# A hybrid attention and retention block on one core: another order of the modulation weights and of the first two token blocks, and later requests for rows and the context copy

## The chip, the cores and the metric

The kernel runs on one core of a Trainium2 chip. The metric is the device time of one execution in microseconds (us). A core has TensorE (PE in the rows, PEld its weight loads), VectorE (DVE), ScalarE (ACT), GpSimd (POOL) and SyncE (SP, which here only issues transfers). Each engine runs its own list of instructions in order; they wait for one another through semaphores.

## The reference

One layer of a diffusion backbone, for 2048 latent tokens and 256 context tokens of width 1024. The part that the change touches is the start: modulation, normalisation and the first columns of the input projection.

```python
mod = jax.nn.silu(c) @ w_ada[i] + b_ada[i]
mod_c = jax.nn.silu(c_ctx) @ w_ada[i] + b_ada[i]
shift, scale, gate = ...
h_lat = _rmsnorm(x, norm_g[i]) * (1.0 + scale) + shift
h_ctx = _rmsnorm(ctx, norm_g[i]) * (1.0 + scale_c) + shift_c
# projections of h_lat and h_ctx by w_in: queries, keys, values, gates
# neighbourhood attention (latent queries also read the context keys), retention,
# one output projection, gated residual, final RMSNorm
```

## The kernel before, in words

All is float32 at the interface. A matrix product runs as three products of rounded halves: an operand is split into a high part (`hhi`, `whi`) and a low part (`hlo`, `wlo`), made by a copy with rounding on ACT and a subtraction on DVE or POOL.

**The front.** The modulation weights come in 16 chunks (u, j) of 0.5 MB; u names a quarter of the channels. `ada_split` splits a chunk, `ada_mm` multiplies it with the silu of c and c_ctx (two rows); a chunk that is not split is multiplied in plain float32 (`silc`, two rows). `ada_row` and `ada_fin` copy the sum of a quarter out, transpose it (`mm<-ident,o`) and write its `mods`. The tokens come in eight blocks of 256 latent tokens (0 to 7) and block 8, the context. For each block `squares` (`sq`) sums squares (ACT, then POOL and DVE into `st`), `colsum` (`cs`) sums over channels on PE (`mm<-one,st`), `rstd` (`rs`) takes the inverse root, `spread` (`sp`) spreads it over partitions on PE (`mm<-ident,t`), `spread_mul` (`mu`) multiplies x by it, `prep_ab` (`ab`) applies scale and shift, `prep_hl` (`hl`) splits into high and low. Blocks 0 and 1 take `prep_first` (`p`, 128 channels k at a time) in place of the last two.

**The windows.** The attention keys (weight columns 512 to 1023, `w01`) are computed in five windows: windows 0 to 3 have two token blocks each, window 4 the context. A window has four units of eight steps, a step being three matmuls (line 363). The results are stored to DRAM as `kS`. The list `PLAN` holds entries (n, action): action is issued once step n has been issued, counted over all windows (32 each); all entries with n = -1 come before the first step. `STEPS` gives the order of units over the steps of window 0 and `LOADS` the order of the first loads. A queue of an engine is thus written out by hand: what stands in `PLAN` between two steps stands between their matmuls on PE.

**The context stage.** After window 4 come four units over context tokens (`CTXU`: weight columns 2560, 2816, 3328, 3072; line 374, 48 matmuls each), whose weights are loaded into `st` and split in turn, and then the latent values. Here stand also: reads of the rows of the first tokens back from DRAM (`raw_piece`, `hhi<-hS` and `hlo<-hS`), and a copy of the context rows to DRAM (`cS`). In window 4 the `kS` stores are issued by ACT, not by SP.

Of the kernel before, what the change touches and what calls it, by code (L numbers as in the profile page):

```python
# [9 lines left out]
F32 = mybir.dt.float32  # L10
# [8 lines left out]
P = 128  # L19
# [39 lines left out]
]  # L59
SPL = [9, 0, 1, 0]  # L60
ALO = [0, 5, 9, 4]
PFL = [3, 0, 0, 1, 0, 3, 1, 3]
STEPS = [0, 1, 2, 0, 1, 3, 2, 3, 2, 0, 3, 1, 1, 3, 0, 3, 2, 3, 0, 0, 2, 1, 1, 1, 1, 2, 3, 2, 2, 0, 3, 0]
WSL = [3, 2]
LEAD = 32
LOADS = [
# [16 lines left out]
def hybrid_kernel(ctx: ExitStack, tc: tile.TileContext, a: dict, out: bass.AP):  # L83
# [24 lines left out]
    sil4 = cst.tile([P, KC, 4], F32R, name="sil4")  # L108
    mods = cst.tile([P, 4, 3, 2, 2], F32, name="mods")
# [145 lines left out]
    def prep_first(k):  # L255
        if k == KC - 1:
            spill.extend((i, u, now[0] + 8) for i in range(2) for u in range(2))
        for i in range(2):
            hi, lo = sub_dst(i)
            A, B = ab(i, k)  # L260
            x = raw[i][k // KH][:, k % KH, :]
            nc.scalar.activation(hi[:, k, :], x, AF.Identity, bias=B, scale=A)
            nc.vector.tensor_scalar(x, x, A, B, ALU.mult, ALU.add)
            eng = nc.gpsimd if PFL[k] >> i & 1 else nc.vector
            eng.tensor_tensor(lo[:, k, :], x, f(hi[:, k, :]), ALU.subtract)
# [27 lines left out]
    def ada_split(u, j):  # L293
        whl[u, j] = []
        for k in range(2):
# [3 lines left out]
            eng = nc.gpsimd if ALO[u] >> j & 1 else nc.vector  # L299
            eng.tensor_tensor(t[:, 1, :], w, f(t)[:, 0, :], ALU.subtract)  # L300
            whl[u, j].append(t)

    def ada_mm(u, j):
        if u not in aps:
            aps[u] = ptile(psm)
        for k in range(2):
            ops = [(silc, wad[4 * u + j][:, k, :])]
# [8 lines left out]
    def ada_row(u):  # L316
        rows[u] = op.tile([P, 2, 512], F32, name="o")[:, 0, :]
        n = 4 if SPL[u] else 2
        (nc.scalar.copy, nc.vector.tensor_copy)[u % 2](rows[u][0:n, :], aps[u][0:n, :])
# [132 lines left out]
    nc.sync.dma_start(silc, a["c2"])  # L452
    nc.scalar.activation(silc, silc, AF.Silu)
    nc.scalar.copy(sil4[:, :, 0:2], silc)
# [10 lines left out]
    for name, *args in LOADS:  # L465
# [4 lines left out]
                ws=lambda g: w01.append(w_split(wr[g], lo=WSL[g])))  # L470
    w01 = []
# [19 lines left out]
    def window(b):  # L491
        units = [u_k(w01, 512 + 256 * g, ct, b) for g in range(2) for ct in range(2)]
        left = [KC] * 4
        for n, u in enumerate(STEPS if b == 0 else [u for u in range(4) for _ in range(KC)]):
            if b == 4 and n == 0:
                env["queue"] = nc.scalar
            if b == 4 and n % 4 == 0:
                raw_piece(n // 4)
            if b == 4 and n == 16:
                wr.append(w_split(wr[2]))  # L500
# [11 lines left out]
    def raw_piece(n):  # L512
        u, k = n // 4, (0, 4, 2, 6)[n % 4]
# [288 lines left out]
    for hl in range(2):  # L802
        nc.sync.dma_start(cS[hl], f(blk[4][hl]))
    for n, (c0, u) in enumerate(CTXU):
# [3 lines left out]
        load_w()  # L808
        unit(u(w0, c0, 8))
# [3 lines left out]
    wo_open()  # L813
# [802 lines left out]
```

## Time and profile before

| what | value |
|---|---|
| three runs | 1373.41, 1373.45, 1375.43 us; median 1373.45 |
| profiled execution | 1372.08 us, span 1370.3 us, so 1.8 us lie around the span |
| window 0, first to last step | 28.1 to 72.7 us |
| window 4 | 150.9 to 162.3 us |
| context units | 162.3 to 196.9 us |

The span runs from the first to the last instruction, and times in rows count from its start. PE is busy in 96% of it, so it is the engine to look at: time in which PE waits, or runs at a lower clock, is time of the kernel, as long as nothing later waits anyway.

### The profile page before, as it was taken

How to read it: one execution, taken by the hardware profiler on the slowest of the kernel's cores; microseconds unless marked ns; L12 is line 12 of the kernel's file. 1: busy time of each engine (PE TensorE's matmuls, PEld its weight loads, DVE VectorE, ACT ScalarE, POOL GpSimd, SP SyncE). 2: the span in 40 equal slices, each digit the busy share in tenths (PEclk: the TensorE clock that was granted, in tenths of full speed). 3: DMA queues.
4: the chain of work that ended last, by engine and by line, in shares of the span. 5: the costliest groups of instructions: out<-in, count | busy, mean ns of one | idle time of the engine just before them, and what ended most of it. 6: DMA issues, size and time to landing. Idle time of an engine off the chain costs nothing.

```text
span 1370.3 us, 23083 instructions
## 1 busy us (share of the span) xinstructions
PE 1313.3 (96%) x8236; PEld 1150.2 (84%) x8236; DVE 826.8 (60%) x1440; ACT 606.5 (44%) x1259; POOL 587.7 (43%) x573
## 2 busy tenths in 40 slices
PE   6989989999999999999999999999999899999997
PEld 2477889887898688998899889889998789888886
DVE  5786246577575665377767777776654633345345
ACT  4454333333532444455556465556642234333332
POOL 4452201445124664445535474655423154444432
PEclk9999999999999999999999999999999999999999
DMA  9386877554868566967687787676538998555533
GB/s 364 129 276 234 292 270 182 176 200 153 312 184 233 216 207 200 277 195 202 166 217 203 208 228 225 173 198 200 156 98 267 273 275 277 169 169 169 161 119 128
DMA packets 197397, 287.25 MB, mean 210 GB/s; under 512 B 17313, under 2 KB 125985, under 8 KB 195746
## 3 DMA queue, kind: packets, MB, share of 16 engines
q1 hardware_dynamic: 164866, 228.35, 55.9%
q10 hardware_dynamic: 32416, 57.42, 11.7%
q8 instruction: 66, 1.08, 0.3%
q14 instruction: 49, 0.40, 0.1%
HBM read 194.48 MB, written 91.23 MB: 208 GB/s over the span
## 4 chain that ended last, share of the span: by engine, by line
PE 51%; DMA 7%; DVE 5%; POOL 3%; ACT 3%; issue 2%; SPq 1%; ACTq 0%; DVEq 0%; POOLq 0%
PE mm L374 12%; PE mm L1457 11%; PE mm L671 5%; PE sS L1017 4%; PE tr L1044 3%; PE mm L363 3%; PE po L1065 3%; PE mm L1180 2%; PE tr L1046 2%; PE po L1067 2%; DMA v<-rvS 1%; PE mm L1369 1%; PE mm L1368 1%; PE mm L1367 1%; DMA woS<-g 1%
## 5 line engine op out<-in xcount | busy, mean ns | idle before, releaser
L374 PE MATMUL mm<-whi,hlo 128*128 128x256 f32 x832 | 228.5, 282 | 0.0
L374 PE MATMUL mm<-whi,hhi 128*128 128x256 f32 x768 | 224.2, 292 | 0.0
L374 PE MATMUL mm<-wlo,hhi 128*128 128x256 f32 x768 | 216.8, 282 | 0.0
L1048 ACT CAST pt<-tr 128x640 fp32r<-128x640 f32 (+1 forms) x128 | 95.7, 747 | 161.7 <-PE tr L1046 159.3
L1054 DVE TENSOR_TENSOR pt<-tr,pt 128x640 fp32r<-128x640 f32 (+1 forms) x128 | 113.9, 890 | 79.1 <-ACT pt L1048 77.9
L374 PEld LDWEIGHTS mm<-whi,hlo 128*128 128x128 f32 x832 | 156.3, 190 | 0.4 <-DMA hlo<-cS 0.3
L1037 POOL TENSOR_SCALAR sp<-sp,stt 128x640 f32<-128x640 f32 (+2 forms) x128 | 103.1, 808 | 106.7 <-DVE stt L1036 80.4
L374 PEld LDWEIGHTS mm<-whi,hhi 128*128 128x128 f32 x768 | 146.2, 190 | 0.0
L374 PEld LDWEIGHTS mm<-wlo,hhi 128*128 128x128 f32 x768 | 146.0, 190 | 0.0
L1026 DVE CUSTOM_DVE_ANT_0 sp<-sS,nb 128x640 f32<-128x640 f32 (+2 forms) x128 | 105.5, 824 | 33.6 <-PE sS L1017 27.2
L1031 ACT ACTIVATE sp<-sp,stt 128x640 f32<-128x640 f32 (+2 forms) x128 | 107.4, 839 | 19.9 <-DVE stt L1026 18.7
L363 PE MATMUL mm<-hlo,whi 128*128 128x512 f32 x256 | 101.2, 395 | 6.6 <-DVE hlo L283 2.3
L625 POOL TENSOR_TENSOR whi<-st,whi 128x512 fp32r<-128x512 f32 x48 | 64.0, 1354 | 101.4 <-ACT whi L624 101.4
L363 PE MATMUL mm<-hhi,whi 128*128 128x512 f32 x256 | 107.0, 418 | 0.0
L1017 PE MATMUL sS<-k,q 128*128 128x256 f32 (+3 forms) x512 | 99.1, 315 | 5.3 <-DVE stt L1026 5.0
L363 PE MATMUL mm<-hhi,wlo 128*128 128x512 f32 x256 | 101.2, 395 | 0.3 <-DVE wlo L347 0.3
L671 PE MATMUL mm<-hhi,whi 128*128 128x512 f32 x336 | 98.2, 395 | 2.6 <-POOL whi L625 2.4
L1457 PE MATMUL mm<-wor,y 128*128 128x512 f32 x384 | 95.7, 398 | 1.9 <-DVE xt L1466 1.1
L1466 DVE TENSOR_TENSOR xt<-mm,xt 128x512 f32<-128x512 f32 x64 | 43.8, 686 | 86.5 <-PE mm L1457 86.4
L1017 PEld LDWEIGHTS sS<-k,q 128*128 128x128 f32 x512 | 82.8, 188 | 12.1 <-DVE stt L1026 8.4
L1457 PE MATMUL mm<-won,y 128*128 128x512 f32 x336 | 89.9, 406 | 0.0
L625 POOL TENSOR_TENSOR wlo<-st,wlo 128x512 fp32r<-128x512 f32 x36 | 53.1, 1474 | 77.7 <-ACT wlo L624 77.7
(258 smaller groups left out, 3065.1 us busy)
## 6 DMA issues: line engine op xcount, KB each, us to landing
st<-in_w_in_dram SPq DMA_DIRECT2D x64, 512.0 KB
q<-qS SPq DMA_DIRECT2D x64, 256.0 KB
hlo<-hS SPq DMA_DIRECT2D x20, 512.0 KB
k<-kS SPq DMA_DIRECT2D x16, 576.0 KB
kS<-o SPq DMA_DIRECT2D x16, 512.0 KB
vB<-o SPq DMA_DIRECT2D x64, 128.0 KB
qS<-o ACTq DMA_DIRECT2D x16, 512.0 KB
woS<-g ACTq DMA_DIRECT2D x32, 256.0 KB
```

The costliest lines, as they stand in the source:

```text
L363: nc.tensor.matmul(pm[:, :n], ww[:, k, cs], h[:, k, :], start=(k == 0 and i == 0), stop=(k == KC - 1 and i == 2))
L374: nc.tensor.matmul(pm[:, t * WG:(t + 1) * WG], h[:, k, o:o + P], ww[:, k, :], start=(k == 0 and i == 0), stop=(k == KC - 1 and i == 2))
L625: nc.gpsimd.tensor_tensor(t[:, 1], r, f(t)[:, 0], ALU.subtract)
L671: nc.tensor.matmul(pm, ww[:, k, :], hh[:, k, :], start=(k == 0 and i == 0), stop=(k == KH - 1 and i == 2))
L1017: nc.tensor.matmul(o, hd["q"][i][:, hl, j * P:(j + 1) * P], k, start=(hl == 0), stop=(hl == 1))
L1026: nc.vector.tensor_tensor_reduce(T["sp"][:, :n], T["s"], nbz[big][:, o:o + n], -1.0, 3e38, ALU.add, ALU.min, T["st"][:, 0:1])
L1031: nc.scalar.activation(sp[:, :n], sp[:, :n], AF.Exp, bias=st[:, 0:1], scale=-1.0, accum_out=st[:, 1:2])
L1037: nc.gpsimd.tensor_scalar(sp[:, :n], sp[:, :n], st[:, 2:3], 0.0, ALU.mult, ALU.add)
L1048: nc.scalar.copy(pt[:, :ng_ + 2, 0, :], tr[:, :ng_ + 2, :])
L1054: nc.vector.tensor_tensor(pt[:, :n, 1, :], tr[:, :n, :], f(pt)[:, :n, 0, :], ALU.subtract)
L1457: nc.tensor.matmul(pm, yy[:, k, :], ww[:, k, sl], start=(k == 0 and i == 0), stop=(k == 3 and i == 2))
L1466: nc.vector.tensor_tensor(xts[t][:, sl], pm, xts[t][:, sl], ALU.add)
```

## The change

1. The start has another order. The modulation weights of quarter 0 are requested ahead of x; other chunks are split ((0,1), (0,3), (3,0) and (3,2) in place of (0,0), (0,3) and (2,0)), and the four of quarter 2 are multiplied unsplit, one after the other. Beside split chunks of its quarter an unsplit one is multiplied with `silz`, silc with two rows of zeros. The tables that gave each split its engine are gone (`ALO`, `PFL`, `WSL`), and the weights `w01` are split half by half.
2. The units of window 0 go round evenly, and `PLAN` has another order up to step 23; from the entry (23, 'cs', 4) on it is the same.
3. In window 4 only the four pieces of `hhi` are read; those of `hlo` follow between the loads of the context units. The context copy is written later, in halves. The split of the 2560 weights takes DVE and not POOL for its low part. `wo_open` (the first gate weights) moves into the values.

```diff
 PLAN = [
...
-    (4, 's', 2, 0), (4, 'x', 4), (4, 'p', 2), (5, 'sq', 2), (7, 'm', 2, 0), (8, 'm', 2, 1), (9, 'p', 3),
...
-    (12, 'p', 5), (12, 'm', 3, 1), (12, 'p', 4), (13, 'sq', 4), (13, 'cs', 2, 3), (13, 'm', 3, 2), (14, 'm', 3, 3),
...
+    (7, 'm', 2, 0), (7, 'm', 2, 1), (7, 'm', 2, 2), (7, 'm', 2, 3), (7, 'sq', 2), (7, 'sq', 3), (7, 'cs', 2, 3),
...
+    (16, 'ab', 2, 0), (17, 'blk', 1), (17, 'ab', 3, 0), (18, 'hl', 2, 0), (19, 'hl', 3, 0), (20, 'sq', 4), (20, 'ab', 2, 1),
+    (21, 'ab', 3, 1), (22, 'hl', 2, 1), (23, 'hl', 3, 1),
...
-SPL = [9, 0, 1, 0]
+SPL = [10, 0, 0, 5]
...
-            if b == 4 and n % 4 == 0:
-                raw_piece(n // 4)
+            if b == 4 and n % 8 == 0:
+                raw_piece(0, n // 8)
             if b == 4 and n == 16:
-                wr.append(w_split(wr[2]))
+                wr.append(w_split(wr[2], lo=0))
...
-    for hl in range(2):
-        nc.sync.dma_start(cS[hl], f(blk[4][hl]))
+
+    def spill_ctx(hl):
+        for u in range(2):
+            ks = slice(u * KH, (u + 1) * KH)
+            nc.sync.dma_start(cS[hl][:, ks, :], f(blk[4][hl])[:, ks, :])
+
     for n, (c0, u) in enumerate(CTXU):
         if n == 3:
             pump.update(y=0, every=4, q=h_sums(T, 0, 1, frows))
         wn = w_split(wcur.pop(0), lo=0)
         load_w()
+        for m in ((0,), (1,), (2, 3), ())[n]:
+            raw_piece(1, m)
+        if n == 3:
+            spill_ctx(0)
         unit(u(w0, c0, 8))
```

How the instructions move, at three places. On DVE, in window 0: before, the sums of squares of block 4 (`st<-st`) stand ahead of the inverse roots of blocks 2 and 3 and of the modulation of quarter 3 (the last `mods` rows).

```order
L200 TENSOR_TENSOR st<-st 128x512
L201 TENSOR_TENSOR st<-st 128x256
L203 TENSOR_TENSOR st<-st 128x256
L214 TENSOR_SCALAR rs<-mm 128x2
L220 COPY t_447<-rs 128x256
L319 COPY o<-mm 2x512
L214 TENSOR_SCALAR rs<-mm 128x2
L220 COPY t_457<-rs 128x256
L329 TENSOR_TENSOR mods<-mm,bada 128x8
L332 SCALAR_TENSOR_TENSOR mods<-mods,ng 128x4
L241 TENSOR_TENSOR hlo<-hlo,mm 128x1024
```

In the changed kernel the same three sums of block 4 stand on DVE behind quarter 3's `mods` and behind the preparation of blocks 0 to 3:

```order
L329 SCALAR_TENSOR_TENSOR mods<-mods,ng 128x4
L261 TENSOR_SCALAR hhi<-hhi,mods 128x256 x2
L263 TENSOR_TENSOR hlo<-hhi 128x256
L261 TENSOR_SCALAR hhi<-hhi,mods 128x256 x2
L263 TENSOR_TENSOR hlo<-hhi 128x256
L239 TENSOR_TENSOR hlo<-hlo,mm 128x1024 x2
L270 TENSOR_SCALAR hlo<-hlo,mods 128x256 x4
L281 TENSOR_TENSOR hlo<-hlo,hhi 128x4x256
L198 TENSOR_TENSOR st<-st 128x512
L199 TENSOR_TENSOR st<-st 128x256
L201 TENSOR_TENSOR st<-st 128x256
```

So they moved from ahead of that work to behind it; on PE the column sum that needs them, `mm<-one,st`, stays behind step 23 in both kernels.

On PE, around the chunks of quarter 2, which in the changed kernel stand in one piece behind step 7, with the column sums of blocks 2 and 3 right behind them:

```order
L360 MATMUL mm<-hhi,wlo 128x512
L308 MATMUL mm<-hlo,silc 2x512 x8
L207 MATMUL mm<-one,st 128x1 x4
L360 MATMUL mm<-hhi,whi 128x512
L360 MATMUL mm<-hlo,whi 128x512
L360 MATMUL mm<-hhi,wlo 128x512
L321 MATMUL mm<-ident,o 128x2 x4
```

Before, the chunks of quarters 2 and 3 stood one or two at a time between steps, and the column sums of blocks 2 and 3 behind step 13.

On SP, from window 4 on: before, the eight row reads, then the loads of the context units' weights (`st<-in_w_in_dram`) with the context copy between them:

```order
L516 DMA hhi<-hS_88 128x1024 x4
L516 DMA hlo<-hS_87 128x1024 x4
L176 DMA st<-in_w_in_dram 128x1024 x2
L803 DMA cS_93<-chi 128x2048
L803 DMA cS_94<-clo 128x2048
L176 DMA st<-in_w_in_dram 128x1024 x10
```

And in the changed kernel:

```order
L521 DMA hhi<-hS_88 128x1024 x4
L174 DMA st<-in_w_in_dram 128x1024 x4
L521 DMA hlo<-hS_87 128x1024
L174 DMA st<-in_w_in_dram 128x1024 x2
L521 DMA hlo<-hS_87 128x1024
L174 DMA st<-in_w_in_dram 128x1024 x2
L521 DMA hlo<-hS_87 128x1024 x2
L174 DMA st<-in_w_in_dram 128x1024 x2
L811 DMA cS_93<-chi 128x1024 x2
```

Of the requests on this queue, those for the weights of two units (3328 and 3072) now follow the `hhi` reads at once; the `hlo` reads and the copy stand behind them.

## Rows read from the trace of the kernel before

**Rows 1.** The page's head.

```profile
span 1370.3 us, 23083 instructions
```

**Rows 2.** By stage: start:end, us, busy time of the engines (instructions), granted clock, DMA share, GB/s.

```profile
60.40:72.70 12.30, 11.93 (x58) 9.77 (x58) 10.92 (x18) 9.09 (x16) 5.50 (x5) 1.00 0.04 13
72.70:97.60 24.90, 22.56 (x102) 18.20 (x101) 21.56 (x31) 13.68 (x19) 11.33 (x8) 1.00 1.03 339
150.90:162.30 11.40, 11.40 (x98) 11.40 (x97) 1.54 (x3) 3.33 (x5) 2.71 (x2) 1.00 0.96 327
162.30:196.90 34.60, 26.49 (x195) 25.39 (x194) 12.74 (x12) 11.76 (x15) 2.04 (x1) 0.90 0.85 304
188.10:193.60 5.50, 5.00 (x21) 4.71 (x22) 4.04 (x4) 3.52 (x4) 0.00 (x0) 0.50 1.03 396
196.90:420.00 223.10, 223.07 (x1378) 199.83 (x1377) 149.73 (x166) 83.41 (x126) 70.79 (x48) 1.00 0.64 202
```

**Rows 3.** Timeline of PE, 70 to 190: start, us, instruction, [idle before, releaser].

```profile
72.72 0.39 PE L363 MATMUL mm<-hhi,whi 128*128 128x512 f32 x1
75.07 0.47 PE L363 MATMUL mm<-hlo,whi 128*128 128x512 f32 x1 [1.96 <-DVE hlo L283]
...
188.13 0.58 PE L374 MATMUL mm<-whi,chi 128*128 128x256 f32 x1 [5.22 <-ACT whi L345]
```

**Rows 4.** Timeline of SP and its DMA issues, 150 to 200.

```profile
155.49 6.60 SPq L516 DMA_DIRECT2D hlo<-hS  x4
...
168.43 0.42 SPq L803 DMA_DIRECT2D cS<-chi  x1
...
182.57 12.16 SPq L176 DMA_DIRECT2D st<-in_w_in_dram  x8
```

**Rows 5.** Waits of SP's queue, 150 to 200: us in total, times, longest.

```profile
SPq L176 <- DMA kS<-o: 17.5, 2, 12.1
```

**Rows 6.** Timeline of ACT and its DMA issues, 150 to 200.

```profile
168.46 0.52 ACTq L151 DMA_DIRECT2D kS<-o  x1
...
182.59 0.60 ACT L443 ACTIVATE o<-mm 128x512 f32<-128x512 f32 x1 [6.04 <-DMA kS<-o]
...
187.03 1.04 ACT L345 CAST whi<-st 128x1024 fp32r<-128x1024 f32 x1 [3.85 <-DMA st<-in_w_in_dram]
```

**Rows 7.** Timeline of PE: one split chunk of modulation, two unsplit ones.

```profile
35.56 1.09 PE L311 MATMUL mm<-o,sil 128*4 128x512 f32 x4
...
48.08 3.60 PE L311 MATMUL mm<-chi,silc 128*2 128x512 f32 x8
```

**Rows 8.** Timeline of DVE, 56 to 78.

```profile
55.69 0.68 DVE L200 TENSOR_TENSOR st<-st 128x512 f32<-128x512 f32 x1
...
60.41 0.16 DVE L332 SCALAR_TENSOR_TENSOR mods<-mods,ng 128x4 f32<-128x4 f32 x1
...
64.02 0.74 DVE L263 TENSOR_SCALAR hhi<-hhi,mods 128x256 f32<-128x256 f32 x2
64.80 0.85 DVE L265 TENSOR_TENSOR hlo<-hhi 128x256 fp32r<-128x256 f32 x1
65.57 2.34 DVE L241 TENSOR_TENSOR hlo<-hlo,mm 128x1024 f32<-128x1024 f32 x2
...
75.45 2.82 DVE L283 TENSOR_TENSOR hlo<-hlo,hhi 128x1024 fp32r<-128x1024 f32 x1
```

**Rows 9.** Timeline of POOL, 53 to 78.

```profile
53.23 1.44 POOL L200 TENSOR_TENSOR st<-st 128x512 f32<-128x512 f32 x1
54.75 0.73 POOL L201 TENSOR_TENSOR st<-st 128x256 f32<-128x256 f32 x1
...
74.35 2.83 POOL L283 TENSOR_TENSOR hlo<-hlo,hhi 128x1024 fp32r<-128x1024 f32 x1 [1.68 <-ACT hhi L279]
```

**Rows 10.** Timeline of ACT, 64 to 76.

```profile
64.14 2.08 ACT L274 ACTIVATE hlo<-hlo,mods 128x256 f32<-128x256 f32 x4 [1.45 <-DVE hlo L241]
...
73.23 1.99 ACT L279 CAST hhi<-hlo 128x1024 fp32r<-128x1024 f32 x2 [0.64 <-DVE hlo L272]
```

More of the change, by code (lines that the diff above doesn't have):

```diff
@@ L39 @@
 PLAN = [
[19 rows of a table removed]
-]
-SPL = [9, 0, 1, 0]
[L61 to L64, printed above, removed]
[20 rows of a table added]
+]
+SPL = [10, 0, 0, 5]
+STEPS = [0, 1, 0, 1, 2, 3, 2, 3, 0, 1, 2, 3, 0, 1, 2, 3, 0, 1, 2, 3, 0, 1, 2, 3, 0, 0, 1, 1, 2, 2, 3, 3]
 LEAD = 32
 LOADS = [
[3 rows of a table removed]
+    ('a', 0, 0), ('a', 0, 1), ('x', 1), ('a', 0, 2), ('a', 0, 3), ('x', 0), ('c',), ('a', 1, 0), ('a', 1, 1), ('w', 0), ('a', 1, 2),
+    ('a', 1, 3), ('w', 1), ('a', 2, 0), ('a', 2, 1), ('x', 2), ('a', 2, 2), ('a', 2, 3), ('x', 3), ('a', 3, 0), ('a', 3, 1), ('a', 3, 2), ('a', 3, 3),
 ]
@@ L108, in hybrid_kernel @@
     sil4 = cst.tile([P, KC, 4], F32R, name="sil4")
+    silz = cst.tile([P, KC, 4], F32, name="silz")
     mods = cst.tile([P, 4, 3, 2, 2], F32, name="mods")
@@ L257, in prep_first @@
             spill.extend((i, u, now[0] + 8) for i in range(2) for u in range(2))
-        for i in range(2):
+        for i in (1, 0):
             hi, lo = sub_dst(i)
@@ L263, in prep_first @@
             nc.vector.tensor_scalar(x, x, A, B, ALU.mult, ALU.add)
-            eng = nc.gpsimd if PFL[k] >> i & 1 else nc.vector
+            eng = nc.gpsimd if i else nc.vector
             eng.tensor_tensor(lo[:, k, :], x, f(hi[:, k, :]), ALU.subtract)
@@ L298, in ada_split @@
             nc.scalar.copy(t[:, 0, :], w)
-            eng = nc.gpsimd if ALO[u] >> j & 1 else nc.vector
-            eng.tensor_tensor(t[:, 1, :], w, f(t)[:, 0, :], ALU.subtract)
+            nc.vector.tensor_tensor(t[:, 1, :], w, f(t)[:, 0, :], ALU.subtract)
             whl[u, j].append(t)
@@ L306, in ada_mm @@
         for k in range(2):
-            ops = [(silc, wad[4 * u + j][:, k, :])]
+            ops = [(silz if SPL[u] else silc, wad[4 * u + j][:, k, :])]
             if SPL[u] >> j & 1:
@@ L318, in ada_row @@
         n = 4 if SPL[u] else 2
-        (nc.scalar.copy, nc.vector.tensor_copy)[u % 2](rows[u][0:n, :], aps[u][0:n, :])
+        nc.scalar.copy(rows[u][0:n, :], aps[u][0:n, :])
     def ada_fin(u):
@@ L452, in hybrid_kernel @@
     nc.sync.dma_start(silc, a["c2"])
+    nc.vector.memset(silz, 0.0)
     nc.scalar.activation(silc, silc, AF.Silu)
+    nc.vector.tensor_copy(silz[:, :, 0:2], silc)
     nc.scalar.copy(sil4[:, :, 0:2], silc)
@@ L469, in hybrid_kernel, with ws_half @@
                 w2=lambda: load_w(), s=ada_split, m=ada_mm, ar=ada_row, af=ada_fin, p=prep_first,
-                ws=lambda g: w01.append(w_split(wr[g], lo=WSL[g])))
-    w01 = []
+                ws=lambda g, u: ws_half(g, u))
+    w01, wps = [], {}
+    def ws_half(g, u):
+        if u == 0:
+            w, wps[g] = w_parts(wr[g])
+            w01.append(w)
+        wps[g][u]()
     def run_acts(n):
@@ L510, in window, with raw_piece @@
                 tick()
-    def raw_piece(n):
-        u, k = n // 4, (0, 4, 2, 6)[n % 4]
+    def raw_piece(u, n):
+        k = (0, 4, 2, 6)[n]
         if k == 0:
@@ L812, in hybrid_kernel @@
     load_w()
-    wo_open()
-    W, mine = values(vunits([([w0], 1024, 0), ([w0], 1024, 1), ([w1], 1280, 0), ([w1], 1280, 1)]), {}, 4)
+    spill_ctx(1)
+    W, mine = values(vunits([([w0], 1024, 0), ([w0], 1024, 1), ([w1], 1280, 0), ([w1], 1280, 1)]), {0: [wo_open]}, 4)
     def take(b):
```

37 rows, old and new, of tables (LOADS, PLAN) are left out of this document.

## The prediction

> **What bounds the kernel now.** I read the windows by stage first. From 196.9 to 420 PE is busy for 223.07 of 223.10 us [rows 2]: nothing there waits for another engine, so whatever time the two stages before it gain or lose is handed on, not swallowed. The change touches only those stages, the front with its windows and the context stage. Two of their rows show lost time. In the context stage PE is busy for 26.49 of 34.60 us at a granted clock of 0.90 [rows 2]. In the front the losses are small: 11.93 busy of 12.30 us at the end of window 0, then 22.56 of 24.90 us in window 1 and a bit beyond [rows 2], with one wait of 1.96 us for the low part that DVE makes at line 283 [rows 3].
>
> Second the timelines of the context stage. Its worst wait is 5.22 us at 188.13, for ACT's split of the 3072 weights [rows 3]. ACT had waited there for the weights (187.03, [rows 6]), which SP had requested only at 182.57 [rows 4]: SP's queue stood for up to 12.1 us waiting for a `kS` store [rows 5]. ACT issued that store at 168.46 and it was done when ACT itself went on at 182.59 after 6.04 us of waiting for it [rows 6], so it took 14 us. In the same stretch the four `hlo` reads had been put on the queue until 162.1 and the context copy from 168.43 on [rows 4]; DMA was busy at 0.96 and 0.85 [rows 2]. After the wait the granted clock is 0.50, the lower level of 1.2 GHz, for the whole row from 188.10 to 193.60 [rows 2].
>
> **The context stage after the change.** Ahead of the requests for the 3328 and 3072 weights SP now has only the four `hhi` reads; the `hlo` reads (2 MB) and the copy (2 MB) come later. The request for 3072 needs the split of 2816, not the last `kS` store. What is to be gained: window 4 takes 11.40 us for 98 matmuls, 0.116 each, where nothing waits [rows 2]; the 195 matmuls of the stage would then take 22.7 us of its 34.60, so 11.9 us at most. The parts of it that hang on the late request are the 5.22 us and the half of 5.5 us at half clock, 2.75, together 8.0. The rest are shorter waits for weights, behind the same stores. I take 11.0, between 8.0 and 11.9, near the upper end because all the traffic that stood ahead of stores and weights moves together. Where does it go? The copy is read back much later, and the `hlo` reads are wanted in the fourth unit, behind DMA at 0.64 share in the long stage that follows [rows 2]; I price their return at nothing, and if that cover were gone, at the 1.2 us that one 0.5 MB piece takes at the 396 GB/s of [rows 2].
>
> **The front after the change.** *Modulation.* One more chunk is split: 1.09 in place of 1.80 (half of 3.60) on PE [rows 7], so 0.7 less. The first chunk waits for no split any more; at most another 1.09, I take 0.5. Quarter 2's four chunks are 7.2 us in one piece, the same work as before. So quarter 3's modulation comes about when it did (60.41, [rows 8]), 1.2 us earlier.
>
> *The new wait.* Counted from quarter 3's `mods`, PE has ten steps up to step 23, and then the column sum of block 4, whose squares now stand behind everything. PE ran 18 steps in the 11.93 us after 60.4 [rows 2], 0.66 each, so it comes there 6.6 us on. The squares come thus, in DVE's order: four scalings and two low parts, 2 x 0.74 + 2 x 0.85 = 3.2; two `mu` 2.34, in all 5.5 [rows 8]. ACT's four scalings of 2.08 [rows 10] end at 6.6, a cast (half of 1.99, [rows 10]) at 7.6. Then POOL and DVE make one low part each. DVE's row of 75.45 is 2.82 long beside POOL's of 74.35, and ends at 78.27 [rows 8, 9]: the pair takes 3.9 us, since the two do not run at once. That is 11.5. The sums of squares are again POOL's 1.44 and 0.73 [rows 9] and DVE's 0.68 and two shorter ones, which I put at 0.43 each by their size against the 0.68 [rows 8]: 3.7 together if they too take turns, 15.2 in all. PE waits 15.2 - 6.6 = 8.6, and with the 0.5 that its transposes stand ahead of the `mods`, 9 us.
>
> *Behind it.* Eight steps remain, 5.3 us. A wait of 5.22 us left 5.5 us of half clock [rows 2, 3], so a wait of 9 does it too: 2.75. The spreading of block 4, whose inverse root stands on DVE behind four more scalings and a low part, I put at 1 us of waiting, between 0 and the 3.9 of that pair. Window 1 would start 15.2 + 5.3 + 2.75 + 1 = 24.2 after 60.41, at 84.7, against 72.72 before [rows 3]: 12.0 later. Against that stand the 1.2 of the modulation and the 1.96 us of [rows 3], since blocks 2 and 3 are long ready by then: 8.9, say **9 us** lost. The bounds: 6.5, if the clock holds and the spreading waits for nothing (-3.75) but modulation gains nothing (+1.2); 11.5, if modulation comes as much later as two new short waits cost (see the third case).
>
> **The sum.** 1372.08 (the profiled execution; 1.8 us of it lie around the span, [rows 1]) + 9 - 11 = 1370.1. The median of the runs is 1.4 above that execution, so 1371.5. A change of 0.2%, 2.7 us, is about what a measurement of this kernel can tell from none.
>
> **Rivals.**
>
> *The front loses less (faster).* The 9 us rest on POOL and DVE taking turns throughout. For it speaks the pair at 74.35 and 75.45; against it, that scalings and `mu` from PSUM may run beside POOL, and that ACT may be further ahead than I let it. If the wait is 5.2 in place of 9 and the clock still falls, the front loses 5: 1373.45 + 5 - 11 = 1367.5 to 1368.
>
> *The store stays late (slower).* Store and reads are on two queues, ACT's and SP's. What I saw is a store that took 14 us while SP's queue was full; that SP's traffic was the cause is my inference. If the store of the last `kS` unit takes 14 us whatever SP does, ACT stands at the result of the 2816 unit as it did at 182.59, the split of 3072 behind it: PE would wait for it some 5 us again and get the low clock for 2.75, so of the 11 only some 4 are regained: 1373.45 + 9 - 4 = 1378.5. It decides once that store takes more than about 11 us. For it speaks that the stores may simply be slow; against it, that most of the traffic beside them goes away. The Trainium skill has a rule for this: on its page "DMA: Bandwidth & Descriptors", section "Queues, rings and completion order", each DMA engine serves the queues that have work in turn, packet by packet. By that a store on ACT's queue would get its share however long SP's queue is, and emptying SP's queue would help it little. The 14 us of [rows 6] for 0.5 MB don't look like half of the bandwidth, so the trace bears this out only in part.
>
> *A second fall of the clock (about no change).* Right behind quarter 2's chunks PE now has the column sums of blocks 2 and 3, whose squares come from ACT, POOL and DVE only then: a pair of sums costs the 3.7 of above, so two waits of 2 to 2.5 us with almost nothing between them. Single waits of 1.96 us left the clock at 1.00 [rows 2, 3], the 5.22 did not; this lies between. A fall there puts some 5.5 us of chunks and steps at half pace, 2.4 to 2.75 later: 1373.45 + 11.5 - 11 = 1374. The Trainium skill, page "TensorE: Matmul & The Clock Gate", section "HAM oscillation — how this bites in real kernels", says that short work between recurring waits starts at the low clock every time; the waits here are of that kind, and no row before has two in a row.
>
> *It doesn't matter.* That both shifts vanish later is excluded by 223.07 of 223.10 [rows 2].
>
> **How the numbers follow.** The forecast has a chance of 0.35, the cheaper front 0.30, the second fall 0.20, the late store 0.15. The range takes the first three and the lower half of the fourth's way: from 1367.5 (context 11, front 5) to 1377 (context 8, front 11.5). Faster by over 0.2% means below 1370.75: a third of the forecast's case and nearly all of the cheaper front, 0.40. Slower, above 1376.2, are the late store and a little of the others, 0.18. The same is the rest, 0.42.
>
> **What would show it.** PE waits some 9 us for `one,st` of block 4 in window 0, at about 67, released by DVE's last sum of squares, and a stretch of granted clock near 0.5 follows; window 1 starts near 84 and has no wait at its first steps. Quarter 3's `mods` are written between 58 and 61. Window 4 starts 9 us later than 150.9. The context units take 23 to 24 us with a granted clock of 1.00 and no wait over 1.5 us; SP requests the 3072 weights before the last `kS` store has landed. Wrong would be the step on the front if window 1 starts before 80, the step on the context if PE waits there for ACT's split by more than 2 us, and the sum if the stages from 197 on wait for `hlo` reads.

## The result, and the profile after

| | median of runs | profiled execution | first step | window 1 | window 4 | values |
|---|---|---|---|---|---|---|
| before | 1371.85 us (11 runs) | 1372.08 | 28.13 | 72.72 | 150.90 | 196.88 |
| after | 1377.52 us (11 runs) | 1378.85 | 29.38 | 87.93 | 166.89 | 202.45 |

The columns on the right are the starts of the first matmul of a stage on PE's timeline. The ratio is 1.0047, interval 1.0029 to 1.0064: the change makes the kernel 4 to 9 us slower. The forecast was 1371.5, its range 1367.5 to 1377. In the two traces window 4 begins 16.0 us later; the context units take 24.26 us in place of 34.59 and give 10.3 back; 5.6 of loss are left where the values begin, and 6.8 at the end.

The windows by stage of the changed kernel (start:end, us, busy time of PE, PEld, DVE, ACT and POOL with instructions, granted clock, DMA share, GB/s):

```profile
44.00:48.00 4.00, 1.47 (x9) 1.39 (x10) 3.03 (x5) 0.23 (x1) 1.48 (x2) 0.93 0.49 182
48.00:52.00 4.00, 4.00 (x14) 2.95 (x14) 1.99 (x7) 1.61 (x3) 1.06 (x2) 0.50 0.00 0
...
78.30:84.00 5.70, 5.65 (x15) 4.66 (x16) 3.92 (x6) 2.58 (x3) 2.60 (x2) 0.50 0.00 0
...
166.90:178.20 11.30, 11.30 (x98) 11.30 (x97) 3.90 (x5) 3.33 (x5) 0.00 (x0) 1.00 0.95 320
178.20:202.50 24.30, 23.29 (x195) 22.88 (x194) 9.00 (x9) 10.32 (x13) 0.00 (x0) 1.00 0.85 306
202.50:420.00 217.50, 216.82 (x1331) 193.70 (x1331) 147.34 (x165) 83.41 (x125) 69.33 (x47) 1.00 0.68 215
```

Against [rows 2]: the context stage (178.2 to 202.5) has 23.29 us of busy PE in 24.30 at a granted clock of 1.00, where it had 26.49 in 34.60 at 0.90. The values still swallow next to nothing (PE busy for 216.82 of 217.50). In the front there are two stretches at 0.50, 48 to 52 and 78.3 to 84; the kernel before has 1.00 at 48 to 52 and in its row of 60.4 to 72.7 [rows 2].

The timeline of PE in the changed kernel (start, us, instruction, [idle before, releaser]):

```profile
45.03 0.61 PE L207 MATMUL mm<-one,st 128*128 128x1 f32 x4 [1.93 <-DVE st L201]
47.14 0.75 PE L207 MATMUL mm<-one,st 128*128 128x1 f32 x4 [1.50 <-DVE st L201]
...
78.35 1.02 PE L207 MATMUL mm<-one,st 128*128 128x1 f32 x4 [8.28 <-DVE st L201]
...
115.59 0.70 PE L360 MATMUL mm<-hlo,whi 128*128 128x512 f32 x1 [2.83 <-POOL hlo L281]
...
185.54 0.38 PE L371 MATMUL mm<-wlo,chi 128*128 128x256 f32 x1 [0.76 <-DVE wlo L344]
```

The first two waits are the column sums of blocks 2 and 3 behind quarter 2's chunks; the clock falls at the second. The third is the new wait for block 4. The last is the longest of the context units, 0.76 us where [rows 3] had 5.22.

The timeline of DVE in the changed kernel, from quarter 3's `mods` to block 4's sums:

```profile
63.49 0.16 DVE L329 SCALAR_TENSOR_TENSOR mods<-mods,ng 128x4 f32<-128x4 f32 x1
...
72.73 2.50 DVE L281 TENSOR_TENSOR hlo<-hlo,hhi 128x1024 fp32r<-128x1024 f32 x1 [1.48 <-ACT hhi L277]
...
77.87 0.43 DVE L201 TENSOR_TENSOR st<-st 128x256 f32<-128x256 f32 x1
...
81.06 2.55 DVE L281 TENSOR_TENSOR hlo<-hlo,hhi 128x1024 fp32r<-128x1024 f32 x1 [1.47 <-ACT hhi L277]
```

From the `mods` to the end of the sums it is 63.49 to 78.30, 14.8 us, where 15.2 was predicted; but the `mods` come 3.1 later than before [rows 8], not 1.2 earlier. The low part of 81.06, still preparation of blocks 2 and 3, will matter below.

The waits of SP's queue in the changed kernel, 165 to 205 (us in total, times, longest):

```profile
SPq L174 <- DVE wlo L344: 23.4, 10, 7.5
```

the timeline of its issues:

```profile
85.42 0.63 SPq L149 DMA_DIRECT2D kS<-o  x1
...
176.51 10.46 SPq L174 DMA_DIRECT2D st<-in_w_in_dram  x4
```

and that of ACT, both of the changed kernel:

```profile
89.51 0.59 ACT L380 CAST o<-mm 128x512 fp32r<-128x512 f32 x1 [4.19 <-DMA kS<-o]
...
180.28 0.37 ACT L380 CAST o<-mm 128x256 fp32r<-128x256 f32 x1 [4.10 <-DMA kS<-o]
...
182.62 0.52 ACTq L149 DMA_DIRECT2D kS<-o  x1
...
191.29 0.60 ACT L440 ACTIVATE o<-mm 128x512 f32<-128x512 f32 x1 [3.73 <-PE mm L371]
...
199.32 0.59 ACT L446 COPY o<-mm 128x512 f32<-128x512 f32 x1 [5.35 <-DMA rkS<-o]
```

The four requests for the 3328 and 3072 weights are issued from 176.51 on, spread over 10.46 us, and what holds them now is the split that frees their buffers (`wlo`), no longer a `kS` store [rows 5]. The last `kS` store of the stage leaves at 182.62, and at the result of the 2816 unit (191.29) ACT waits for PE, where it had waited for that store [rows 6]. ACT does wait for a store one unit later (199.32), but PE waits for nothing there. The issue at 85.42 stores the first result of window 0.

### The profile page after: what moved, and what is told of

Read it like the earlier page. It is cut to its first block, busy times and chain, and to the rows that moved or that the text cites. A ratio compares the mean times of both kernels' runs of the same rounds, so it can differ in the third digit from the quotient of the medians.

```text
span 1377.1 us, 23099 instructions
## 1 busy us (share of the span) xinstructions
PE 1318.7 (96%) x8236; PEld 1153.9 (84%) x8236; DVE 834.6 (61%) x1445; ACT 608.4 (44%) x1263; POOL 582.8 (42%) x570
## 4 chain that ended last, share of the span: by engine, by line
PE 64%; DMA 10%; DVE 8%; ACT 4%; issue 3%; POOL 3%; SPq 2%; ACTq 0%; DVEq 0%; POOLq 0%
PE mm L371 16%; PE mm L676 13%; PE mm L1470 11%; PE mm L360 5%; PE sS L1030 4%; PE tr L1057 3%; PE po L1078 3%; PE mm L1193 2%; PE tr L1059 2%; PE po L1080 2%; DMA kS<-o 1%; DMA v<-rvS 1%; PE mm L1382 1%; PE mm L1381 1%; PE mm L1380 1%
## 5 line engine op out<-in xcount | busy, mean ns | idle before, releaser
L1039 DVE CUSTOM_DVE_ANT_0 sp<-sS,nb 128x640 f32<-128x640 f32 (+2 forms) x128 | 105.5, 825 | 33.1 <-PE sS L1030 27.7
```

The lines of the kernel that those rows point to most:

```text
L1039: nc.vector.tensor_tensor_reduce(T["sp"][:, :n], T["s"], nbz[big][:, o:o + n], -1.0, 3e38, ALU.add, ALU.min, T["st"][:, 0:1])
```

## The experiments

All fifteen by stage. A profile is one execution; the ratio is that of the timed runs against the kernel before, with its interval. e14 is e6 timed again. The fences with edits show the entries and lines that matter, not the whole difference.

| kernel | first step | window 1 | window 4 | values | context units | ratio |
|---|---|---|---|---|---|---|
| e1, part 3 alone | 28.25 | 74.42 | 153.33 | 189.00 | 24.28 | 0.9954 (0.9935 to 0.9972) |
| e2, parts 1 and 2 | 29.47 | 86.06 | 166.75 | 210.96 | 32.89 | 1.0085 (1.0063 to 1.0107) |
| e6, rows later | 27.24 | 73.45 | 151.41 | 186.85 | 24.05 | 0.9940 (0.9922 to 0.9958) |
| e14, the same | 26.98 | 71.66 | 150.58 | 185.83 | 23.86 | 0.9934 (0.9908 to 0.9960) |
| e7, copy later | 28.00 | 74.25 | 153.37 | 191.60 | 26.85 | 0.9959 (0.9942 to 0.9976) |
| e3, squares early | 28.72 | 86.55 | 164.30 | 200.16 | 24.67 | 1.0028 (1.0012 to 1.0044) |
| e5, filling matmuls | 28.89 | 85.63 | 162.94 | 197.19 | 23.06 | 0.9995 (0.9982 to 1.0008) |
| e3b, sums early too | 29.35 | 74.91 | 161.24 | 196.60 | 24.16 | 1.0020 (1.0007 to 1.0034) |
| e4, and 2, 3 later | 32.72 | 74.95 | 162.68 | 198.66 | 24.78 | 1.0013 (1.0001 to 1.0026) |
| e8, old `STEPS` | 29.04 | 85.17 | 163.88 | 201.35 | 26.27 | 1.0075 (1.0049 to 1.0100) |
| e10, e3b, old `STEPS` | 28.98 | 73.98 | 161.18 | 196.92 | 24.44 | 1.0044 (1.0027 to 1.0060) |
| e9, new start alone | 31.69 | 81.26 | 160.47 | 198.03 | 26.37 | 0.9997 (0.9982 to 1.0013) |
| e11, squares late alone | 27.00 | 77.89 | 155.29 | 200.16 | 33.48 | 1.0023 (1.0007 to 1.0040) |
| e12, low parts later | 29.07 | 75.45 | 153.84 | 189.00 | 23.97 | 0.9945 (0.9924 to 0.9966) |
| e13, e12, old `STEPS` | 29.76 | 76.29 | 155.16 | 190.26 | 23.90 | 0.9940 (0.9912 to 0.9967) |

### The two halves: e1 and e2

e1 is the kernel before with part 3 of the change; e2 the changed kernel with part 3 undone.

> The kernel before with the third part of the change alone (rows and context copy requested later, the 2560 weights' low part on DVE, the gate weights opened in the values). Theory, the loss is all in the front and the context part keeps its gain by itself: context units take 24 to 25 us in place of 34.6, no wait of PE there over 1 us, granted clock 1.00, and the time falls by 9.5 to 11 us (ratio 0.992 to 0.993). Rival, the context stage gained only because the front came 16 us later and left the queues emptier: under 6 us, with a kS store still over 11 us on its way and a wait for ACT's split left.

> The changed kernel with the third part undone. Theory, the parts add up: window 4 starts 16 us later than in the kernel before, the context units take 34 to 35 us with the wait of some 5 us and the low clock, and the time is 15 to 17 us above the kernel before (ratio 1.011 to 1.0125). Rival, the context stage's loss was partly owed to the old front: under 12 us.

The halves are separate: the context units take 24.28 us with the rows and the copy later, 32.89 without. By time part 3 gives 0.46%, the front costs 0.85%, and their sum, 0.39%, lies within the interval of the whole change. Both times are smaller than I expected (0.7 to 0.8% of gain, 1.1 to 1.25% of loss). With the old context stage the units took 34.59, 32.89 and 33.48 us (before, e2, e11), so the 10.3 us that the pair of before and after shows is at the upper end; the rest of the shortfall is not explained. In e2 the waits for weights are back, though none is as long as the 5.22 of before:

```profile
185.91 0.39 PE L371 MATMUL mm<-whi,chi 128*128 128x256 f32 x1 [1.52 <-ACT whi L342]
...
202.42 0.39 PE L371 MATMUL mm<-whi,chi 128*128 128x256 f32 x1 [2.35 <-ACT whi L342]
```

### Rows or copy: e6, e14, e7

e6 is before with the `hlo` reads between the loads of the context units and the copy where it was; e7 is before with the copy at the end and the reads where they were. Both have the small edits of part 3 as well: the low part of the 2560 weights on DVE, the copy written in halves, the gate weights opened in the values.

```diff
e6
-                raw_piece(n // 4)
+                raw_piece(0, n // 8)
...
+        for m in ((0,), (1,), (2, 3), ())[n]:
+            raw_piece(1, m)
e7
+        if n == 3:
+            spill_ctx(0)
...
+    spill_ctx(1)
```

> The kernel before with only the reads of the hlo rows moved between the context units' loads; the context copy is written ahead of the units as before. Theory, the reads delayed the first two stores (and so ACT's split of the 2816 weights), the copy delayed the last one (and so the wait of 5.2 us): the short waits of 1.4 and 0.8 us at the second unit go, a wait of 2 to 5 us for ACT's split of the 3072 weights stays; the context units take 28 to 33 us. Rival, the reads alone did it: 24 to 25 us.

> The kernel before with only the context copy moved behind the context units' loads; all eight row reads stay in window 4. Theory: the last store is no longer late, the wait of 5.2 us and the low clock go, the short waits at the second unit stay; the context units take 25.5 to 27.5 us. Rival, the reads alone did it: over 31 us.

> The fastest version so far again, with more rounds: the kernel before with only the hlo row reads moved between the context units' loads. Context part alone by its profile 10 us, so a ratio of 0.992 to 0.995 to the kernel before; if what the later stages give back is systematic and not scatter, 0.996 or more.

PE's longest wait in the context units of e6:

```profile
169.72 0.39 PE L374 MATMUL mm<-wlo,chi 128*128 128x256 f32 x1 [0.76 <-DVE wlo L347]
```

and of e7:

```profile
171.86 0.38 PE L374 MATMUL mm<-whi,chi 128*128 128x256 f32 x1 [1.18 <-ACT whi L345]
```

With either of the two moves the long wait is gone; with the rows later all of the 10.3 us are gained (24.05), with the copy later 7.7 (26.85). My theory for e6 fell, its rival held; for e7 the theory held. That the small edits, which both have, are not the cause is argued and not shown by a run: the only one of them that PE waited for was POOL's low part of the 2560 weights, for 0.27 us in the kernel before,

```profile
164.39 0.39 PE L374 MATMUL mm<-wlo,chi 128*128 128x256 f32 x1 [0.27 <-POOL wlo L347]
```

and the late requests of before were released by `kS` stores [rows 5], not by POOL.

### The squares of block 4: e3 and e5

```diff
e3
-(20, 'sq', 4)
+(11, 'sq', 4)      behind (11, 'mu', 3, 0)
e5
+(23, 'pad')        ahead of (23, 'cs', 4)
+        for _ in range(m):
+            nc.tensor.matmul(pm, w01[0][0][:, 0, 0:P], blk[0][0][:, 0, :], start=True, stop=True)
```

e5 puts 26 matmuls, whose results are thrown away, into the wait.

> The changed kernel with the squares of block 4 moved ahead of quarter 3's modulation, nothing else. Theory, the wait of 8.3 us for the column sum of block 4 is the place of these squares in DVE's and POOL's order: that wait goes. But the inverse root of block 4 still stands on DVE behind two more low parts, so a wait of 4 to 7 us for its spreading takes its place, and window 1 starts only 2 to 6 us sooner than in the changed kernel. Rival, the place doesn't matter since PE waits for quarter 3's modulation anyway: under 1 us.

> The changed kernel with 26 matmuls of 512 columns (6 us, results thrown away) put ahead of the column sum of block 4, where PE waits 8.3 us, so that the clock does not fall. Prediction's step, the low clock behind this wait costs 2.75 us: window 1 starts 2 to 2.8 us sooner than 88.6. Theory now, the spreading of block 4 comes when DVE has made its inverse root (84.8), whatever pace PE has until then: the clock stays at 1.00, PE waits some 2 us for the spreading instead, and window 1 starts 0.3 to 1.2 us sooner.

In e3 the sums come in time, and PE stands at the next thing, the spreading, for as long; window 1 starts only 1.4 us sooner, less than the 2 to 6 expected:

```profile
81.69 1.22 PE L225 MATMUL mm<-ident,t 128*128 128x128 f32 x4 [8.32 <-DVE t L218]
```

The inverse root (entry 24, `rs`) stands on DVE behind the same preparation. In e5 a wait of 2.56 us was left, and the clock fell behind it all the same, to 0.50:

```profile
76.59 0.58 PE L207 MATMUL mm<-one,st 128*128 128x1 f32 x4 [2.56 <-DVE st L201]
...
78.50:80.50 2.00, 2.00 (x6) 1.61 (x5) 1.29 (x1) 1.25 (x2) 2.00 (x1) 0.50 0.00 0
```

So e5 does not price the clock by itself. By the ratios its time is some 7 us better than that of the changed kernel. Window 4 begins 4.0 sooner, but 2.0 of this were there ahead of the filling matmuls (quarter 3's `mods` at 61.54 for 63.49); from the `mods` to window 1 it takes 24.1 us, the changed kernel 24.4. The rest is not explained.

### What stays when the waits of window 0 are gone: e3b, e10, e4, e8

```diff
e3b = e3 and
-(23, 'cs', 4), (24, 'rs', 4)
+(15, 'cs', 4), (16, 'rs', 4)      ahead of (16, 'ab', 2, 0)
e4 = e3b and
-(7, 'cs', 2, 3), (8, 'rs', 2), (8, 'rs', 3), (9, 'sp', 2, 3), (11, 'mu', 2, 0), (11, 'mu', 3, 0)
+(11, 'cs', 2, 3), (11, 'rs', 2), (11, 'rs', 3), (13, 'sp', 2, 3), (13, 'mu', 2, 0), (13, 'mu', 3, 0)
e10 = e3b, e8 = the changed kernel, each with STEPS of before
```

> As the run before, and the column sum and inverse root of block 4 moved ahead of the preparation of blocks 2 and 3 too (steps 15 and 16 in place of 23 and 24). Theory: both waits go and with them the low clock behind them, 8.3 + 2.7 us; window 1 then waits again for the low parts of blocks 2 and 3, some 2 to 4 us, so it starts 7 to 10 us sooner than in the changed kernel, and the time is 1367 to 1370 by the kernel before at 1372. Rival, the front is bound by POOL and DVE taking turns: the wait moves to window 1 as a whole, under 4 us gained.

> The changed kernel with block 4's squares, column sum and inverse root ahead as in the run with both, and the column sums of blocks 2 and 3 moved from behind step 7 to behind step 11, so that PE has four steps in hand while ACT, POOL and DVE add up their squares. Theory, the waits of 1.9 and 1.5 us behind quarter 2's chunks and the low clock behind them made quarter 3's modulation late: PE waits under 1 us there, the granted clock stays above 0.9 from 40 to 56 us, quarter 3's modulation is written 2 to 4 us sooner than 63.5, and window 4 starts 2 to 5 us sooner than in the run with both moved. Rival, the modulation comes late because its chunks are loaded late or the start takes longer: under 1 us.

> The changed kernel with the order of units in window 0 as before (STEPS), nothing else. In the changed order the four units end within the last eight steps, and ACT then waits 4.2 us for a kS store before it can take the fourth result, with the squares of block 5 behind it. Theory: with the old order the first results leave earlier, that wait goes, and the 3 us that windows 1 to 3 lose against the kernel before shrink to under 1.5; window 4 starts 1.5 to 3 us sooner than in the changed kernel. Rival, those 3 us come from the low parts and squares of blocks 4 and 5, which stand in the same order on DVE and POOL either way: under 1 us.

> The run with block 4's squares, column sum and inverse root moved ahead, with the order of units in window 0 as before (STEPS) added. In that run window 1 lost 7 us again between its second and its thirteenth step: a wait of 2.2 us for the low parts of block 3, a low clock behind it and a wait of 3.2 us for the squares of block 5, which on DVE stand behind the results of four units that all end in the last eight steps. Theory: with the old order the results leave earlier, the squares of block 5 are in time, and window 1 loses under 3.5 us in place of 7; window 4 starts 3 to 5 us sooner than in that run. Rival, the low parts and the clock set it, whatever the units' order: window 1 still loses 5.5 us or more.

In e3b window 1 starts at 74.91, 13 us sooner than in the changed kernel, but window 4 only 5.7 sooner: window 1 now loses 7.0 us between its 2nd and its 13th step, against before. PE in e3b:

```profile
81.08 0.47 PE L360 MATMUL mm<-hlo,whi 128*128 128x512 f32 x1 [2.17 <-DVE hlo L281]
...
90.65 0.58 PE L207 MATMUL mm<-one,st 128*128 128x1 f32 x4 [3.16 <-DVE st L201]
```

First a low part of blocks 2 and 3 is late, then the squares of block 5, with the low clock between. The old `STEPS` change nothing of it: e10 loses 6.8 there, and e8's windows 1 to 3 take 78.7 us, in the changed kernel 79.0, so that its window 4 comes 3.0 sooner, as expected, but not for the reason that I gave. In e8 the waits at the sums and the spreading of blocks 2 and 3 were shorter in all (2.1 us for 3.8) and the clock held behind them, though it had fallen ahead of them (0.87 from 28 to 36, 0.84 from 36 to 40); its quarter 3's `mods` come 32.2 us after the first step, in the changed kernel 34.1, before 32.3:

```profile
46.55 0.61 PE L207 MATMUL mm<-one,st 128*128 128x1 f32 x4 [0.53 <-DVE st L201]
...
51.18 0.71 PE L225 MATMUL mm<-ident,t 128*128 128x128 f32 x4 [1.54 <-DVE t L218]
```

e4 takes the waits for these sums away altogether, and the `mods` come 31.3 after the first step; but its first step came 3.3 later than in the changed kernel, so that neither the `mods` nor window 4 came sooner as I had expected, and a split chunk is now waited for:

```profile
49.36 0.95 PE L207 MATMUL mm<-one,st 128*128 128x1 f32 x8
...
56.06 1.00 PE L308 MATMUL mm<-o,sil 128*4 128x512 f32 x3 [1.96 <-DVE o L297]
```

Its time is that of e3b within the intervals.

### The place of the preparation of blocks 2 and 3: e12, e13, and e11, e9

What is late in window 1 stands on ACT and DVE behind the preparation of blocks 2 and 3, which the change puts at entries 16 to 23, ahead of the first results of window 0; before, it stood at 24 to 29, among them. (That `PLAN` is the same from the entry (23, 'cs', 4) on, as said above the prediction, is not so: these entries are gone from there.) e12 is e3 with these entries put back, e13 the same with the old `STEPS`. e11 is before with the squares of block 4 late and nothing else; e9 is the changed kernel with the order of before from step 4 on and its `STEPS`.

```diff
e12 = e3 and
-(16, 'ab', 2, 0), (17, 'blk', 1), (17, 'ab', 3, 0), (18, 'hl', 2, 0), (19, 'hl', 3, 0), (20, 'ab', 2, 1), (21, 'ab', 3, 1),
-(22, 'hl', 2, 1), (23, 'hl', 3, 1)
+(24, 'ab', 2, 0), (24, 'ab', 3, 0), (26, 'ab', 2, 1), (26, 'blk', 1), (28, 'hl', 2, 0), (28, 'ab', 3, 1), (28, 'hl', 3, 0),
+(29, 'hl', 2, 1), (29, 'hl', 3, 1)
e11
-(13, 'sq', 4)
+(23, 'sq', 4)
```

> The kernel before with one thing alone: the squares of block 4 moved from step 13 to step 23, right ahead of their column sum. Theory: DVE and POOL come to them only behind the spreading of blocks 2 and 3 (67.9), 3.7 us of taking turns more, so PE waits 4.5 to 6 us at about 67, the clock falls behind it, and window 4 starts 5 to 9 us later than in the kernel before: ratio 1.004 to 1.007. Rival, the wait is taken back at window 1, which waits 2.3 us anyway, and the rest is small: under 3 us, ratio under 1.002.

> The changed kernel with block 4's squares ahead, and everything from the scaling of blocks 2 and 3 on as in the kernel before (column sum of block 4 at 23, low parts of blocks 2 and 3 at 28 and 29, behind the first results on DVE and ACT). Theory: in the runs so far the results of window 0 stood on DVE and ACT behind these low parts, the first kS store was issued at 81 in place of 71, and ACT then waited 6 us for a store with the squares of block 5 behind it. With the old order of this piece window 1 (second to thirteenth step) loses under 2.5 us against the kernel before in place of 7, and window 4 starts 4 to 8 us later than in the kernel before in place of 10. Rival, the chain of DVE and POOL is late as a whole whatever its order: 8 us or more.

> The same with the order of units in window 0 as before too, so that the first results leave earlier still. Theory: as the run with low parts later or up to 2 us sooner at window 4, the first kS store before 76. Rival, as there: 8 us or more later than the kernel before at window 4.

> The changed kernel with the first and the third part (other chunks split, quarter 2 unsplit, modulation weights requested ahead of x, halves of the first weights, entries up to step 3 as changed; rows and copy later), but with the order of the kernel before from step 4 on and its STEPS. Theory, the start itself costs 1 to 2.5 us (first step at 29.4 in place of 28.1, a low clock at 16 to 22) and the rest of the front's loss is the order: quarter 3's modulation at 60 to 62.5, window 4 starts 1 to 4 us later than in the kernel before, the time is 1363 to 1367 by the kernel before at 1372. Rival, the modulation as changed is the loss: quarter 3's modulation after 63, window 4 starts over 8 us later.

The timelines of SP, ACT and PE in e10, whose window 0 has no wait for block 4 any more:

```profile
80.62 0.63 SPq L149 DMA_DIRECT2D kS<-o  x1
...
84.51 0.59 ACT L380 CAST o<-mm 128x512 fp32r<-128x512 f32 x1 [6.13 <-DMA kS<-o]
84.99 2.01 ACT L196 ACTIVATE st<-hhi 128x1024 f32<-128x1024 f32 x2
...
89.49 0.58 PE L207 MATMUL mm<-one,st 128*128 128x1 f32 x4 [2.92 <-DVE st L201]
```

The same places in e12:

```profile
71.81 0.63 SPq L150 DMA_DIRECT2D kS<-o  x1
...
77.36 0.47 PE L361 MATMUL mm<-hlo,whi 128*128 128x512 f32 x1 [1.40 <-DVE hlo L282]
...
77.67 2.01 ACT L197 ACTIVATE st<-hhi 128x1024 f32<-128x1024 f32 x2
...
86.36 0.50 PE L208 MATMUL mm<-one,st 128*128 128x1 f32 x4
```

and in the kernel before:

```profile
71.00 0.63 SPq L151 DMA_DIRECT2D kS<-o  x1
```

With the preparation ahead of the results, the first result is stored at 80.62; ACT, wanting the result buffer again, stands 6.13 us for a store, the squares of block 5 (84.99) behind it, and PE waits 2.92 for these. With the preparation among the results the store leaves at 71.81, the squares run at 77.67, and the column sum at 86.36 waits for nothing. Window 1 then loses 1.0 us (e12) and 0.0 (e13) on the stretch where e3b lost 7.0; e1, e7 and e14, with the old front, have up to 1.0 there too. Window 4 of e12 begins at 153.84, close to the 150.6 to 153.4 of before, e1, e6, e7 and e14, and its time is that of e1.

Two lengths sum this up. From quarter 3's `mods` to window 1 it takes 12.3 us in each of before, e1, e6, e7 and e14; 23.5 to 24.4 in the changed kernel, e2, e3, e5 and e8; 18.9 in e11; and 12.6 to 13.6 in e3b, e10, e12 and e13. From the first step to window 4 it takes 122.8 to 125.4 with the old front, 137.5 in the changed kernel, 131.9 in e3b, 124.8 in e12 and 125.4 in e13. So but for the first step, which stays later, the front's loss hangs on two places: block 4's squares behind the preparation, and the preparation ahead of the results. e12 has the two waits behind quarter 2's chunks too (1.90 and 1.50 us, the clock at 0.62 from 48 to 52), and its `mods` come 32.8 after the first step, within the 32.3 to 34.0 of the old front.

e11 shows the first place by itself: a wait of 3.06 us, shorter than I expected, and a clock of 0.50 behind it from 68.2 to 74; window 4 begins 5.5 later than in before, counted from the first step. Its time is 0.23% longer, less than the 0.4 to 0.7% expected.

```profile
68.27 1.02 PE L209 MATMUL mm<-one,st 128*128 128x1 f32 x4 [3.06 <-DVE st L203]
```

In e9 the `mods` came at 68.11 and window 4 9.6 us later than before, as its rival had it, but it decides nothing on the start: a split chunk that its order makes late was waited for by itself, and the first step came at 31.69, later than in all others with the new start but e4.

```profile
60.63 0.88 PE L308 MATMUL mm<-o,sil 128*4 128x512 f32 x2 [3.84 <-DVE o L297]
```

## Why the prediction was wrong

**The context stage was right.** 10.3 us of gain where 11 was forecast, within 8.0 to 11.9; granted clock 1.00, longest wait 0.76, the requests as described. What the working left open, which of the two moves counts, e6 and e7 answer: either, so far as the small edits that both have are not the cause. The late store did not come, and that its 1378.5 lies close to the measured time is luck. At 191.29 ACT stands for no store: the last `kS` store, issued at 182.62, was done within 8.7 us, where it had taken 14, below the 11 us at which that rival was to decide. Where ACT does wait for a `kS` store, at the start of the stage, nothing changed: 4.10 us at 180.28 where before had

```profile
164.59 0.37 ACT L383 CAST o<-mm 128x256 fp32r<-128x256 f32 x1 [4.13 <-DMA kS<-o]
```

though the `hlo` reads were gone from SP's queue. The Trainium skill, page "DMA: Bandwidth & Descriptors", section "Queues, rings and completion order", says that each DMA engine serves the queues that have work in turn. The wait at 180.28 agrees with what the prediction made of that, since fewer reads beside the store did not shorten it; the last store, 14 us before and at most 8.7 after, does not. The prediction also took the last store for 0.5 MB; a store that ACT issues there has half of that, by the transfers of the kernel before from 150 to 205:

```profile
kS<-o ACTq DMA_DIRECT2D x4, 256.0 KB
```

**The step that failed** is "So quarter 3's modulation comes about when it did". It was priced 1.2 us earlier and came 3.1 later (63.49 for 60.41), 4.3 in all, and window 1, to start at 84.7 less the 1.2, 83.5, started at 87.93. 1.25 of the 4.3 is the first step, which had no term. With the new start it comes at 28.7 to 29.8 (32.72 in e4, 31.69 in e9), with the old one at 27.0 to 28.3. Ahead of it the granted clock is low in the changed kernel (first row) and not in the kernel before (second row):

```profile
16.00:20.00 4.00, 2.79 (x13) 2.44 (x14) 3.16 (x7) 1.26 (x3) 2.01 (x2) 0.59 1.03 410
...
16.00:20.00 4.00, 4.00 (x17) 1.43 (x16) 0.98 (x4) 0.24 (x1) 0.71 (x1) 1.00 1.03 411
```

That this clock is what makes the step late was not tested by itself. The other 3.0 lie between the first step and the `mods`, which take 34.1 us where 31.1 were priced. There the third rival, with a chance of 0.20, came true: the waits at 45.03 and 47.14, and 0.50 of clock from 48 to 52. e4, which has neither, takes 31.3. The Trainium skill, page "TensorE: Matmul & The Clock Gate", section "HAM oscillation — how this bites in real kernels", says that short work between recurring waits starts at the low clock each time. The changed kernel's trace agrees (waits of 1.93 and 1.50 us, then 0.50).

But part of the 3.0 is the luck of two executions. Up to the `mods` e1, e6, e7 and e14 have the order of before, e2 and e5 that of the changed kernel. From the first step to the `mods` the old order takes 32.3 to 34.0 us, the mean 33.3, the new one 32.6 to 34.1, the mean 33.1: the profile of before is the fastest of its kind, that of the changed kernel the slowest. By these means the new order gains 0.2 in place of 1.2 and the first step comes 1.5 later, so that the step was off by 2.6 rather than 4.3.

**The terms behind it were sized well:** 14.8 us from the `mods` to the end of the sums (15.2 predicted), a wait of 8.28 (9), 9.6 from there to window 1 (5.3 + 2.75 + 1 = 9.05), and window 1's first wait gone, 2.2 (1.96).

**A term was missing.** I counted the 1.96 us of window 1 as the end of the matter, "since blocks 2 and 3 are long ready by then", and asked for the early preparation only what it delays ahead of block 4's sums. It also delays the results of window 0 on DVE and ACT, their stores, and through these block 5. In the changed kernel, where window 1 starts late, little of it shows: beside the 2.2 us gained by the wait that is gone, windows 1 to 3 lose some 3 (4.7 in e2, 1.3 in e5). The wait of 2.83 at 115.59, 1.70 before, is among them; that it comes of the early preparation is not shown, since e3 has 1.45 there with it and e13 2.59 without. What the early preparation costs there is seen once the first wait is removed: of the 7 us of e3b 3.16 are the wait for block 5 and 2.17 that for its own low part, with the low clock between. It goes when the preparation is put back (e12, e13). That is also why undoing the late squares alone (e3, e3b) gets back so little.

**The sum:** 1372.08 + 16.0 - 10.3 is 1377.8 by the stages, the profiled execution took 1378.85, and the front's 16.0 against the forecast's 9 is nearly the whole error: 4.3 by the late modulation, 3.0 by windows 1 to 3. Two slips in the working weigh little: 12.0 - 1.2 - 1.96 is 8.8 and not 8.9, and 0.5 MB at 396 GB/s take 1.3 us and not 1.2. The last 1.1 us come later than 202 and are within what two profiles differ by there.

**A version that beats both** is e6, the kernel before with the `hlo` reads later, the small edits of part 3 and nothing of the front: 0.9940 and 0.9934 in two measurements. e1, e12 and e13 (0.9954, 0.9945, 0.9940) beat both too, and their intervals overlap with those of e6.

## What to carry to other kernels

When a piece of preparation is moved ahead in a hand-written order, price not only who waits for what now stands behind it, but also the results that the same engines must still copy out: a result that leaves late holds its buffer, and the engine stands at that buffer with the next block's work behind it. Removing the first wait that such a move causes may only uncover the next; put the move itself back before concluding what it cost. A stretch of transfers that is wanted late is worth moving off a queue which someone waits on, and one of two such transfers may be enough.

## What the runs showed of the hardware

The same waits do not always bring the clock down. Two stretches of the kernel before and of e1, whose front has the same order of instructions, have these rows, the waits ahead of them first; that ahead of the second stretch of before is the 1.96 us of [rows 3]. Before:

```profile
38.59 0.50 PE L363 MATMUL mm<-hlo,whi 128*128 128x512 f32 x1 [1.71 <-DVE hlo L265]
...
40.50:44.00 3.50, 3.50 (x10) 0.91 (x9) 2.22 (x3) 0.00 (x0) 0.83 (x1) 1.00 1.02 407
78.40:80.50 2.10, 2.08 (x9) 1.76 (x10) 2.10 (x3) 0.00 (x0) 1.76 (x2) 1.00 1.02 398
```

e1:

```profile
38.71 0.50 PE L363 MATMUL mm<-hlo,whi 128*128 128x512 f32 x1 [1.75 <-DVE hlo L265]
...
76.78 0.47 PE L363 MATMUL mm<-hlo,whi 128*128 128x512 f32 x1 [1.97 <-DVE hlo L283]
...
40.50:44.00 3.50, 3.50 (x6) 0.92 (x5) 2.33 (x4) 0.00 (x0) 0.82 (x1) 0.55 1.03 411
78.40:80.50 2.10, 2.10 (x7) 1.62 (x6) 2.10 (x2) 0.92 (x1) 2.10 (x2) 0.50 0.93 317
```

PE was busy throughout in both, and in e1 did the work at 0.55 and 0.50. Counted from the first step, window 4 begins after 122.8 us with neither fall (before), 123.6 with a fall behind the second wait alone (e14), 124.2 behind the first alone (e6), and 125.1 and 125.4 with both (e1, e7). So what followed a single wait of 1.7 to 2.0 us cost 0.8 to 1.4 us in one execution and nothing in another. The executions of the kernel before reach from 1365.6 to 1378.7: a difference of 3 us at one stage of one profile says little here without a wait that explains it.
